# Modulation rows ahead of the input, values by pairs of token tiles, and input tiles read by grid rows

## The chip, the cores and the metric

The kernel runs on one core of one Trainium2 chip. Five engines work side by side, each through its own list of instructions in order: TensorE (PE; its weight loads are listed as PEld), VectorE (DVE), ScalarE (ACT), GpSimd (POOL) and SyncE (SP). Transfers are issued from SP's and ACT's lists and carried by 16 transfer engines. The metric is the time of one launch in microseconds.

## The reference, cut to what matters

The kernel does one step of a two-layer trunk: 512 latent tokens (a grid of 8 rows and 64 columns) and 128 context tokens, 1024 features. What the change touches is the start of layer 0: the modulation, the first norm and the projection to values.

```
def rmsnorm(x, g):
    y = x * lax.rsqrt(jnp.mean(x * x, axis=-1, keepdims=True) + EPS)
    return y * g

def adaln(cond, w, b):
    m = jax.nn.silu(cond) @ w + b
    return jnp.split(m[..., None, :], 6, axis=-1)

# layer 0: c for the latents, c_ctx for the context
sh, sc, ... = adaln(c, ada_w[0], ada_b[0])
h = rmsnorm(x, norm_mix_pre[0]) * (1.0 + sc) + sh
q, k, v = jnp.split(h @ na_w_qkv[0], 3, axis=-1)
```

Everything else (neighbourhood attention, the output projection, the FFN with its convolution, the second layer) is the same in both kernels.

## The kernel before, in words

The 640 tokens are five tiles of 128, x0 to x3 of latents and x4 of context. A latent tile holds 16 columns of the grid with all 8 rows, and a token's place in it is column times 8 plus row. `x_load` issues the load of a tile (512 KB, 128 partitions of 4 KB); `raw_ap` gives the source's counts and steps, from the outside in. `x_norm` squares the tile on ACT (with a sum), forms the reciprocal root on POOL in two small instructions and scales the tile on DVE. `x_turn` turns it on PE in eight transposes of 128x128 (`tr`), four to a PSUM bank; ACT copies the first bank to `xT` and DVE the second. `xT` has the features on the partitions in 8 chunks k, and 640 tokens along.

The modulation of the first norm (a scale and a shift of 1024 each) comes in four pieces i of two chunks k. `mod_load` loads a piece as four tiles `wf` of 512 KB; there are seven buffers `wf`, so the last tile of the third piece must wait until the second piece's first tile has been used, and the fourth piece for the rest. `mod_rows` multiplies (`row`), ACT copies the row (`rs`), and `mod_cols` turns it to columns on PE (`col`); three small instructions of DVE make the columns of scale and shift, `gcol` and `hcol`. Then for both k of the piece ACT writes scale times `xT` plus shift, rounded, to the high part `hT[0]`, DVE computes the same in full into `xT`, and DVE writes the difference to the low part `hT[1]`.

The values of the first four heads are `v_part(k, tiles)`: for a k and a tile three matmuls of 256 columns (high x high, high x low, low x high) into the tile's bank `vp`, for which `wv_load` loads half of the weights (512 KB, tile `wr`), ACT casts them (`wh`) and DVE subtracts (`wl`). Five `vp` banks of eight are held from the start.

PE's order is the order of the code, since `pe` ties each PE instruction to the one before it. The other engines' lists are set by a scheduler from the dependencies. In the kernel before SP issues x0, the constants (`const_loads`), x1 to x4, the first piece of modulation, the first value weights, pieces 2 and 3, the second value weights and piece 4. PE turns all five tiles, then does `row` and `col` of piece 1, `row` of piece 2, and then values, columns and rows in turn, until the weights of the queries and keys follow.

Of the kernel before, what the change touches and what calls it, by code (L numbers as in the profile page):

```python
# [104 lines left out]
def hybrid_step(ctx: ExitStack, tc: tile.TileContext, A, O):  # L105
# [13 lines left out]
    def turn(*a, **k):  # L119
        pe(nc.tensor.transpose(*a, **k))  # L120
# [4 lines left out]
    def f32(t):  # L125
        return t.bitcast(F32)
# [16 lines left out]
    cc = wp.tile([40, P], F32, tag="wr", name="cc")  # L143

    def const_loads():
        nc.sync.dma_start(cc[0:8, :], A["c"].rearrange("o (k p) -> (o k) p", p=P))
        nc.sync.dma_start(cc[8:16, :], A["c_ctx"].rearrange("(k p) -> k p", p=P))
        nc.sync.dma_start(cc[16:32, :], A["ada_b"][0, 0:2048].rearrange("(k p) -> k p", p=P))
        nc.sync.dma_start(cc[32:40, :], A["norm_mix_pre"][0].rearrange("(k p) -> k p", p=P))
        nc.sync.dma_start(ident, A["k_ident"])  # L150

    mhalf = cst.tile([P, 1], F32, name="mhalf")
    nc.gpsimd.memset(mhalf, -0.5)
    scolp = cst.tile([P, 2 * KC + 30], F32, name="scolp")
# [351 lines left out]
    with ExitStack() as s:  # L506
        sp = s.enter_context(pool("st"))
        xts = []

        def x_load(t):  # L510
            xt = sp.tile([P, D], F32, name=f"x0_{t}")
            if t < 4:
                nc.sync.dma_start(xt, raw_ap(A["x_sample"], 16 * t * D, [[D, 16], [GW * D, 8], [1, D]]))
            else:
                nc.sync.dma_start(xt, x_in(t))
            xts.append(xt)

        x_load(0)
        const_loads()
# [12 lines left out]
        gcol = sp.tile([P, KC, 2], F32, name="gcol")  # L532
        hcol = sp.tile([P, KC, 2], F32, name="hcol")

        def x_norm(t):
            xt = xts[t]
            ss = sm.tile([P, 1], F32, name="ss")
            junk = sp.tile([P, D], BF16, tag="junk", name="junk0")
            nc.scalar.activation(junk, xt, AF.Square, accum_out=ss)
            r = rstd_of(ss, D)  # L540
            nc.vector.tensor_scalar(xt, xt, r, None, op0=ALU.mult)

        def x_turn(t):
            for q in range(2):
                tr = bk.get("tr")
                tv = tr.rearrange("p (a b) -> p a b", a=4)
                for j in range(4):
                    turn(tv[:, j, :], xts[t][:, (4 * q + j) * P : (4 * q + j + 1) * P], ident)
                dst = xT[:, 4 * q : 4 * q + 4, t * P : t * P + P]
                if q:  # L550
                    nc.vector.tensor_copy(dst, tv)
                else:
                    nc.scalar.copy(dst, tv)
                bk.put(tr)

        def mod_load(i):
            out = {}
            for n in range(2):
                for h in range(2):
                    out[n, h] = sp.tile([P, 4, 256], F32, tag="wf", name="wf", bufs=7)  # L560
                    nc.sync.dma_start(out[n, h], rows(A["ada_w"][0], 4 * h, 4, D - D * n + 256 * i, 256))
            return out

        def mod_rows(i, ws):


            row = bk.get("row")
            for (n, h), w in ws.items():
                for j in range(4):
                    k = 4 * h + j  # L570
                    mm(row[32 * j : 32 * j + 32, 256 * n : 256 * n + 256], scolp[:, 2 * k : 2 * k + 32],
                       w[:, j, :], start=h == 0, stop=h == 1)
            rs = sp.tile([P, 512], F32, tag="rs", name="rs")
            nc.scalar.copy(rs, row)
            bk.put(row)
            return rs

        def mod_cols(i, rs):

            col = bk.get("col")  # L580
            for n in range(4):
                mm(col[:, 2 * n : 2 * n + 2], rs[:, n * P : n * P + P], sel, start=True, stop=True)
            cv = col[:, 0:8].rearrange("p (a b) -> p a b", b=2)
            ks = slice(2 * i, 2 * i + 2)

            def bc(c0):
# [3 lines left out]
            nc.vector.tensor_mul(gcol[:, ks, :], gcol[:, ks, :], bc(16))  # L590
            nc.vector.tensor_add(hcol[:, ks, :], cv[:, 2:4, :], bc(0))
            bk.put(col)
            for k in (2 * i, 2 * i + 1):
                for q, cs in ((0, slice(0, NS)), (1, slice(NS, T))):
                    g1, h1 = gcol[:, k, q : q + 1], hcol[:, k, q : q + 1]
                    i0 = nc.scalar.activation(hT[0][:, k, cs], xT[:, k, cs], AF.Identity, bias=h1, scale=g1)
                    nc.vector.tensor_scalar(xT[:, k, cs], xT[:, k, cs], g1, h1, op0=ALU.mult, op1=ALU.add)
                i1 = nc.vector.tensor_sub(hT[1][:, k, 0:T], xT[:, k, :], f32(hT[0][:, k, 0:T]))
            normed[:] = i0, i1

        vts_of[0] = na_v_tile()
        loads, wv = {}, {}

        def wv_load(i):
            wv[i] = wsplit(rows(wqkv, 4 * i, 4, 2048, 256), 4, 256)

        def x_in_norm(ts):
            for t in ts:
                if t:
                    x_load(t)  # L610
                x_norm(t)

        x_in_norm(range(NT))
        loads[0] = mod_load(0)
        wv_load(0)
        loads[1] = mod_load(1)
        loads[2] = mod_load(2)
        wv_load(1)
        loads[3] = mod_load(3)
        na_v_cache(vts_of[0], 0)  # L620
        vb = [bk.get("vp") for _ in range(NT)]

        def v_part(k, cs):
            for c in cs:
                wh, wl = wv[k // 4]
# [12 lines left out]
        rs = mod_rows(2, loads[2])  # L638
        v_part(2, range(3))
        mod_cols(2, rs)  # L640
        v_part(2, range(3, NT))
        v_part(3, range(NT))
        rs = mod_rows(3, loads[3])
        v_part(4, range(3))
        mod_cols(3, rs)
        v_part(4, range(3, NT))
        v_part(5, range(NT))
# [1314 lines left out]
```

## Time and profile before

| | |
|---|---|
| median of 3 runs | 1548.12 us (1547.24 to 1548.54) |
| span of the profiled execution | 1546.0 us |
| median less span | 2.1 us |
| PE busy | 1512.8 us, 98% |
| DVE, ACT, POOL busy | 66%, 55%, 45% |
| moved by the transfer engines | 243.99 MB, mean 158 GB/s |

The page gives no time of its own for the profiled execution beside its span from the first to the last instruction; what lies around the span is the 2.1 us to the median of the runs. Times in the profile are counted in us from the span's start. In a row of the timeline stand start, length, engine, line, operation, what is written and read, how many instructions were merged (x), and in brackets how long the engine had been idle and who ended that. L117 and L120 are the helpers through which all matmuls and transposes go, so the tile's name tells what is done. In a group of instructions the busy time and the mean of one in ns stand behind the bar. "Under 512 B" in a row on packets counts packets of that size or smaller steps up to the next limit; loads of 4 KB rows have one packet for each row.

### The profile page before, as it was taken

Reading aid. Unit: us, or ns where it says so; the run is one execution under the profiler, and the core shown is the slowest. Engines: PE = TensorE matmul, PEld = TensorE weight load, DVE = VectorE, ACT = ScalarE, POOL = GpSimd, SP = SyncE. Lnnn points to the kernel's source line nnn. Section 1 sums busy time; section 2 is a strip of 40 time slices with the busy share of each in tenths; the row PEclk is TensorE's granted clock in tenths of the full one; section 3 lists DMA queues with packets and bytes.
Section 4 is the critical chain, followed back from the end, with each engine's and each line's share of the span. In section 5 each row is a group of like instructions: output and inputs, shape, how many; then the busy total and the mean of one; then the engine's idle time right before and its main releaser. Section 6 shows DMA issues by size and latency. Waiting matters only on the chain.

```text
span 1546.0 us, 26097 instructions
## 1 busy us (share of the span) xinstructions
PE 1512.8 (98%) x9709; PEld 1344.4 (87%) x9709; DVE 1024.1 (66%) x1648; ACT 854.2 (55%) x1624; POOL 701.8 (45%) x606
## 2 busy tenths in 40 slices
PE   6999999999999999999999999999999999999998
PEld 5988998888999999978887878878899999988886
DVE  4553453659877666756757877773988887786554
ACT  5665564646655555654544447763666655554443
POOL 1554463432355455525444464532235666542433
PEclk9999999999999999999999999999999999999999
DMA  9745454253565665388574421015433334447664
GB/s 318 210 122 159 122 132 116 64 190 124 183 224 177 221 190 162 114 277 272 178 234 155 129 69 42 2 40 190 153 114 115 119 111 156 132 164 252 226 221 131
DMA packets 196666, 243.99 MB, mean 158 GB/s; under 512 B 11484, under 2 KB 153020, under 8 KB 196540
## 3 DMA queue, kind: packets, MB, share of 16 engines
q1 hardware_dynamic: 186704, 235.74, 47.7%
q10 hardware_dynamic: 9836, 6.59, 2.5%
q8 instruction: 76, 1.25, 0.3%
q14 instruction: 50, 0.41, 0.1%
HBM read 214.38 MB, written 26.34 MB: 156 GB/s over the span
## 4 chain that ended last, share of the span: by engine, by line
PE 66%; DVE 5%; ACT 2%; issue 2%; POOL 1%; DMA 1%; POOLq 0%; DVEq 0%; ACTq 0%
PE acc L117 19%; PE ux L117 18%; PE uz L117 8%; PE gp L117 5%; PE uy L117 4%; PE po L117 3%; PE y L117 3%; PE s L117 2%; PE tp L120 2%; PE ada L117 1%; DMA wr<-in_ffn_w_up 1%; DVE t L1281 1%; ACT gp L1692 1%; PE tr L120 0%; DVE xo L400 0%
## 5 line engine op out<-in xcount | busy, mean ns | idle before, releaser
L180 POOL TENSOR_TENSOR wl<-wr,wh 128x1024 fp32r<-128x1024 f32 x70 | 173.3, 2480 | 238.5 <-ACT wh L178 223.5
L1204 POOL TENSOR_TENSOR wl<-wr,wh 128x1024 fp32r<-128x1024 f32 x76 | 183.5, 2435 | 46.9 <-ACT wh L1203 43.3
L117 PE MATMUL ux<-B,wh 128*128 128x322 f32 x832 | 200.1, 311 | 0.9 <-ACT u L1258 0.9
L1281 DVE SCALAR_TENSOR_TENSOR t<-C,cw,t 128x644 f32<-128x644 f32 x176 | 156.3, 888 | 51.3 <-ACT t L1279 50.7
L117 PE MATMUL acc<-wh,alo 128*128 128x512 f32 x440 | 172.3, 392 | 0.3 <-DVE alo L1173 0.3
L178 ACT CAST wh<-wr 128x1024 fp32r<-128x1024 f32 x140 | 145.6, 1048 | 48.5 <-DMA wr<-in_ffn_w_down 37.4
L117 PE MATMUL acc<-wh,ahi 128*128 128x512 f32 x440 | 171.9, 391 | 0.0
L117 PE MATMUL acc<-wl,ahi 128*128 128x512 f32 x440 | 171.8, 391 | 0.0
L117 PE MATMUL uz<-B,wh 128*128 128x322 f32 x640 | 156.2, 312 | 0.9 <-ACT v L1258 0.9
L117 PEld LDWEIGHTS ux<-B,wh 128*128 128x128 f32 x832 | 143.6, 189 | 3.4 <-issue 1.2
L1173 DVE TENSOR_TENSOR alo<-ain,ahi 128x384 fp32r<-128x384 f32 (+1 forms) x88 | 84.0, 973 | 84.9 <-ACT ahi L1171 84.0
L117 PE MATMUL ux<-B,wl 128*128 128x322 f32 x416 | 129.5, 311 | 2.7 <-DVE wl L1204 2.7
L117 PE MATMUL qk<-hT,wh 128*128 128x384 f32 (+1 forms) x512 | 122.4, 315 | 0.0
L117 PEld LDWEIGHTS uz<-B,wh 128*128 128x128 f32 x640 | 110.9, 189 | 4.3 <-ACT v L1258 1.5
L1204 POOL TENSOR_TENSOR vl<-wr,vh 128x1024 fp32r<-128x1024 f32 x38 | 96.3, 2535 | 24.6 <-ACT vh L1203 24.3
L1203 ACT CAST wh<-wr 128x1024 fp32r<-128x1024 f32 x84 | 84.8, 1049 | 40.8 <-DVE wr L1227 40.5
L1279 ACT ACTIVATE t<-C,cw 128x644 f32<-128x644 f32 x88 | 78.6, 893 | 47.8 <-DVE C L1309 40.3
L180 DVE TENSOR_TENSOR wl<-wr,wh 128x1024 fp32r<-128x1024 f32 x70 | 91.3, 1315 | 20.1 <-ACT wh L178 19.5
L117 PE MATMUL uz<-B,wl 128*128 128x322 f32 x320 | 99.6, 311 | 0.3 <-POOL wl L1204 0.3
L117 PEld LDWEIGHTS acc<-wh,alo 128*128 128x128 f32 x440 | 82.5, 188 | 18.8 <-DVE alo L1173 1.1
L117 PEld LDWEIGHTS acc<-wl,ahi 128*128 128x128 f32 x440 | 82.6, 188 | 17.9
L117 PEld LDWEIGHTS acc<-wh,ahi 128*128 128x128 f32 x440 | 82.6, 188 | 17.8
(259 smaller groups left out, 3857.7 us busy)
## 6 DMA issues: line engine op xcount, KB each, us to landing
wr<-in_ffn_w_up SPq DMA_DIRECT2D x88, 512.0 KB
wr<-in_ffn_w_down SPq DMA_DIRECT2D x88, 512.0 KB
wr<-in_ada_w SPq DMA_DIRECT2D x72, 512.0 KB
act<-act SPq DMA_DIRECT2D x44, 321.0 KB
wr<-in_na_w_qkv SPq DMA_DIRECT2D x24, 512.0 KB
mod<-modrow SPq DMA_DIRECT2D x20, 512.0 KB
ain<-act SPq DMA_DIRECT2D x44, 192.0 KB
wf<-in_ada_w SPq DMA_DIRECT2D x16, 512.0 KB
```

What stands on the lines that cost most here:

```text
L117: pe(nc.tensor.matmul(*a, **k))
L120: pe(nc.tensor.transpose(*a, **k))
L178: i = nc.scalar.copy(hi, raw)
L180: j = (low or nc.vector).tensor_sub(lo, raw, f32(hi))
L1173: pin(nc.vector.tensor_sub(lo[:, 0 : c1 - c0], ain[:, 0 : c1 - c0], f32(hi[:, 0 : c1 - c0])))
L1203: nc.scalar.copy(hl[0], src)
L1204: low.tensor_sub(hl[1], src, f32(hl[0]))
L1279: nc.scalar.activation(t, taps(0), AF.Identity, bias=cw[:, 3, n : n + 1], scale=cw[:, 1, n : n + 1])
L1281: nc.vector.scalar_tensor_tensor(t, taps(d), cw[:, w, n : n + 1], t, op0=ALU.mult, op1=ALU.add)
L1692: nc.scalar.activation(self.pt[i].rearrange("p (a b) -> p a b", a=2), sv, AF.Exp, bias=nm, scale=-1.0, accum_out=su)
```

## The change

Three things are changed.

- The loads of the constants move from SP's to ACT's list, to its very start. SP begins with the first piece of modulation, then x0, x1, the first value weights, x2, x3, x4; the rest follows as it was. `row` and `col` of piece 1 stand ahead of the first turn.
- A latent tile is read by grid rows: 8 rows of the grid outside, 16 columns inside, so 64 KB lie together in the source, and a token's place in the loaded tile is row times 16 plus column. The turn writes its columns with a step of 8 to bring the former order back.
- `mod_cols` ends with `gcol` and `hcol`; what follows is `mod_apply(i, parts)`, which can be done for a range of tokens. For piece 1 it is done for tiles 0 and 1, 2 and 3, and 4, and the value matmuls of k = 0 and 1 follow by these groups. Pieces 2 to 4 are applied whole. A `vp` bank is taken when its tile's first value matmul is due.

On PE the list begins with one product for the constants and the five tiles' turns; then come the first two `row`:

```order
L120 MATMUL ct<-ident,cc 128x40
L120 MATMUL tr<-ident,x_0_134 128x128 x8
...
L120 MATMUL tr<-ident,x_4_193 128x128 x8
L117 MATMUL row<-wf,scolp 32x256 x16
L117 MATMUL col<-sel,rs 128x2 x4
L117 MATMUL row<-wf,scolp 32x256 x16
L117 MATMUL vp<-wh,hT_122 128x256
```

The same place in the changed kernel:

```order
L120 MATMUL ct<-ident,cc 128x40
L117 MATMUL row<-wf,scolp 32x256 x16
L117 MATMUL col<-sel,rs 128x2 x4
L120 MATMUL tr<-ident,x_0_161 128x8x16 x8
L120 MATMUL tr<-ident,x_1_171 128x8x16 x8
L120 MATMUL tr<-ident,x_2_187 128x8x16 x8
L117 MATMUL vp<-wh,hT_127 128x256
...
L120 MATMUL tr<-ident,x_3_197 128x8x16 x8
L120 MATMUL tr<-ident,x_4_207 128x128 x8
L117 MATMUL vp<-wh,hT_127 128x256
...
L117 MATMUL row<-wf,scolp 32x256 x16
L117 MATMUL col<-sel,rs 128x2 x4
L117 MATMUL row<-wf,scolp 32x256 x16
```

The first `row` and `col` moved ahead of the turns. Twelve value matmuls (tiles 0 and 1) stand between turn 2 and turn 3, and eighteen (tiles 2, 3 and 4) between turn 4 and the second `row`. Behind that `row` come its `col` and the third `row` with no value matmul between them.

ACT's list in the changed kernel, from the first copied row on; `junk,ss` is the square of a tile, `xT` the copy of half a turned tile, `wh` the cast of the value weights:

```order
L574 COPY rs<-row 128x512
L538 ACTIVATE junk_164,ss<-x_0_161 128x1024
L538 ACTIVATE junk_174,ss<-x_1_171 128x1024
L553 COPY xT<-tr 128x4x128
L179 CAST wh<-wr 128x1024
L553 COPY xT<-tr 128x4x128
L538 ACTIVATE junk_190,ss<-x_2_187 128x1024
L602 ACTIVATE hT_127<-xT,hcol,gcol 128x256 x2
L538 ACTIVATE junk_200,ss<-x_3_197 128x1024
L553 COPY xT<-tr 128x4x128
L538 ACTIVATE junk_210,ss<-x_4_207 128x1024
L553 COPY xT<-tr 128x4x128
```

In the kernel before, the squares of x0 to x2 stood one behind the other, and the cast behind all five turns and the first copied row. Now the square of x2 stands behind the copies of turns 0 and 1 and the cast.

DVE's list in the changed kernel, behind the scaling of x3 and x4: the copies of turns 3 and 4, and between and behind them what `mod_apply` does for tiles 2, 3 and 4:

```order
L551 COPY xT<-tr 128x4x128
L603 TENSOR_SCALAR xT<-xT,gcol,hcol 128x256
L551 COPY xT<-tr 128x4x128
L604 TENSOR_TENSOR hT_128<-xT,hT_127 128x256
L603 TENSOR_SCALAR xT<-xT,gcol,hcol 128x256
L603 TENSOR_SCALAR xT<-xT,gcol,hcol 128x128
L604 TENSOR_TENSOR hT_128<-xT,hT_127 128x256
L604 TENSOR_TENSOR hT_128<-xT,hT_127 128x128
L603 TENSOR_SCALAR xT<-xT,gcol,hcol 128x128
L604 TENSOR_TENSOR hT_128<-xT,hT_127 128x128
```

In the kernel before, this work was four pieces and two of 640 columns, in whole rows behind `gcol`, which came after all turns. Seven of these pieces now follow the copy of turn 4.

The diff, cut to its core:

```
     def const_loads():
-        nc.sync.dma_start(cc[0:8, :], A["c"].rearrange("o (k p) -> (o k) p", p=P))
...
-        nc.sync.dma_start(ident, A["k_ident"])
-
+        nc.scalar.dma_start(cc[0:8, :], A["c"].rearrange("o (k p) -> (o k) p", p=P))
...
+        nc.scalar.dma_start(ident, A["k_ident"])
+
+    const_loads()
...
             if t < 4:
-                nc.sync.dma_start(xt, raw_ap(A["x_sample"], 16 * t * D, [[D, 16], [GW * D, 8], [1, D]]))
+                nc.sync.dma_start(xt, raw_ap(A["x_sample"], 16 * t * D, [[GW * D, 8], [D, 16], [1, D]]))
...
                 for j in range(4):
-                    turn(tv[:, j, :], xts[t][:, (4 * q + j) * P : (4 * q + j + 1) * P], ident)
+                    out = tv[:, j, :].rearrange("p (c r) -> p r c", r=8) if t < 4 else tv[:, j, :]
+                    turn(out, xts[t][:, (4 * q + j) * P : (4 * q + j + 1) * P], ident)
...
             bk.put(col)
+
+        def mod_apply(i, *parts):
+
             for k in (2 * i, 2 * i + 1):
-                for q, cs in ((0, slice(0, NS)), (1, slice(NS, T))):
-                    g1, h1 = gcol[:, k, q : q + 1], hcol[:, k, q : q + 1]
-                    i0 = nc.scalar.activation(hT[0][:, k, cs], xT[:, k, cs], AF.Identity, bias=h1, scale=g1)
-                    nc.vector.tensor_scalar(xT[:, k, cs], xT[:, k, cs], g1, h1, op0=ALU.mult, op1=ALU.add)
-                i1 = nc.vector.tensor_sub(hT[1][:, k, 0:T], xT[:, k, :], f32(hT[0][:, k, 0:T]))
+                for c0, c1 in parts:
+                    for q, cs in ((0, slice(c0, min(c1, NS))), (1, slice(max(c0, NS), c1))):
+                        if cs.start >= cs.stop:
+                            continue
...
+                    i1 = nc.vector.tensor_sub(hT[1][:, k, c0:c1], xT[:, k, c0:c1], f32(hT[0][:, k, c0:c1]))
...
-        x_in_norm(range(NT))
         loads[0] = mod_load(0)
+        x_in_norm(range(2))
         wv_load(0)
+        x_in_norm(range(2, NT))
         loads[1] = mod_load(1)
...
-        for t in range(NT):
+        def v_pair(cs):
+            for k in range(2):
+                v_part(k, cs)
+
+        mod_cols(0, mod_rows(0, loads[0]))
+        for t in range(3):
             x_turn(t)
-        rs = mod_rows(0, loads[0])
-        mod_cols(0, rs)
+            if t == 1:
+                mod_apply(0, (0, 256))
+        v_pair((0, 1))
+        for t in range(3, NT):
+            x_turn(t)
+            mod_apply(0, (256, NS) if t < 4 else (NS, T))
+        v_pair((2, 3))
+        v_pair((4,))
+        whole = (0, T)
         rs = mod_rows(1, loads[1])
-        v_part(0, range(2))
         mod_cols(1, rs)
-        v_part(0, range(2, NT))
-        v_part(1, range(NT))
...
+        mod_apply(1, whole)
+        for i in (2, 3):
+            rs = mod_rows(i, loads[i])
+            v_part(2 * i - 2, range(3))
+            mod_cols(i, rs)
+            mod_apply(i, whole)
+            v_part(2 * i - 2, range(3, NT))
+            v_part(2 * i - 1, range(NT))
```

More of the change, by code (lines that the diff above doesn't have):

```diff
@@ L145, in const_loads @@
     def const_loads():
-        nc.sync.dma_start(cc[0:8, :], A["c"].rearrange("o (k p) -> (o k) p", p=P))
-        nc.sync.dma_start(cc[8:16, :], A["c_ctx"].rearrange("(k p) -> k p", p=P))
-        nc.sync.dma_start(cc[16:32, :], A["ada_b"][0, 0:2048].rearrange("(k p) -> k p", p=P))
-        nc.sync.dma_start(cc[32:40, :], A["norm_mix_pre"][0].rearrange("(k p) -> k p", p=P))
-        nc.sync.dma_start(ident, A["k_ident"])
+        nc.scalar.dma_start(cc[0:8, :], A["c"].rearrange("o (k p) -> (o k) p", p=P))
+        nc.scalar.dma_start(cc[8:16, :], A["c_ctx"].rearrange("(k p) -> k p", p=P))
+        nc.scalar.dma_start(cc[16:32, :], A["ada_b"][0, 0:2048].rearrange("(k p) -> k p", p=P))
+        nc.scalar.dma_start(cc[32:40, :], A["norm_mix_pre"][0].rearrange("(k p) -> k p", p=P))
+        nc.scalar.dma_start(ident, A["k_ident"])
+    const_loads()
     mhalf = cst.tile([P, 1], F32, name="mhalf")
@@ L516, in x_load @@
             xts.append(xt)
-        x_load(0)
-        const_loads()
         sel = sp.tile([P, 2], F32, name="sel")
@@ L592, in mod_cols @@
             bk.put(col)
+        def mod_apply(i, *parts):
             for k in (2 * i, 2 * i + 1):
-                for q, cs in ((0, slice(0, NS)), (1, slice(NS, T))):
-                    g1, h1 = gcol[:, k, q : q + 1], hcol[:, k, q : q + 1]
-                    i0 = nc.scalar.activation(hT[0][:, k, cs], xT[:, k, cs], AF.Identity, bias=h1, scale=g1)
-                    nc.vector.tensor_scalar(xT[:, k, cs], xT[:, k, cs], g1, h1, op0=ALU.mult, op1=ALU.add)
-                i1 = nc.vector.tensor_sub(hT[1][:, k, 0:T], xT[:, k, :], f32(hT[0][:, k, 0:T]))
+                for c0, c1 in parts:
+                    for q, cs in ((0, slice(c0, min(c1, NS))), (1, slice(max(c0, NS), c1))):
+                        if cs.start >= cs.stop:
+                            continue
+                        g1, h1 = gcol[:, k, q : q + 1], hcol[:, k, q : q + 1]
+                        i0 = nc.scalar.activation(hT[0][:, k, cs], xT[:, k, cs], AF.Identity, bias=h1, scale=g1)
+                        nc.vector.tensor_scalar(xT[:, k, cs], xT[:, k, cs], g1, h1, op0=ALU.mult, op1=ALU.add)
+                    i1 = nc.vector.tensor_sub(hT[1][:, k, c0:c1], xT[:, k, c0:c1], f32(hT[0][:, k, c0:c1]))
             normed[:] = i0, i1
@@ L608, in x_in_norm @@
             for t in ts:
-                if t:
-                    x_load(t)
+                x_load(t)
                 x_norm(t)
-        x_in_norm(range(NT))
         loads[0] = mod_load(0)
+        x_in_norm(range(2))
         wv_load(0)
+        x_in_norm(range(2, NT))
         loads[1] = mod_load(1)
@@ L620, in hybrid_step @@
         na_v_cache(vts_of[0], 0)
-        vb = [bk.get("vp") for _ in range(NT)]
+        vb = {}
         def v_part(k, cs):
             for c in cs:
+                if k == 0:
+                    vb[c] = bk.get("vp")
                 wh, wl = wv[k // 4]
@@ L627, in v_part @@
                        (wh[:, k % 4, :], wl[:, k % 4, :]), k == 0, k == KC - 1)
-        for t in range(NT):
-            x_turn(t)
-        rs = mod_rows(0, loads[0])
-        mod_cols(0, rs)
+        def v_pair(cs):
[3 more added lines that the diff above has]
+        for t in range(3):
+            x_turn(t)
+            if t == 1:
[7 more added lines that the diff above has]
+        whole = (0, T)
         rs = mod_rows(1, loads[1])
-        v_part(0, range(2))
         mod_cols(1, rs)
-        v_part(0, range(2, NT))
-        v_part(1, range(NT))
[L638 to L647, printed above, removed]
+        mod_apply(1, whole)
[6 more added lines that the diff above has]
+            v_part(2 * i - 1, range(NT))
         crs = []
```

## The prediction

> **What bounds the kernel now.** I read the page first, then the busy time by stretches of the start, then the timeline of the first 50 us, then the transfers there.
>
> ```profile
> span 1546.0 us, 26097 instructions
> PE 1512.8 (98%) x9709; PEld 1344.4 (87%) x9709; DVE 1024.1 (66%) x1648; ACT 854.2 (55%) x1624; POOL 701.8 (45%) x606
> ...
> 9.60:21.40 11.80, 9.64 (x44) 7.91 (x48) 5.58 (x8) 6.80 (x13) 3.46 (x9) 1.00 1.06 330
> 21.40:30.50 9.10, 7.12 (x87) 4.42 (x87) 5.28 (x11) 4.29 (x7) 0.00 (x0) 1.00 1.09 383
> 30.50:50.80 20.30, 20.30 (x204) 17.99 (x204) 13.95 (x32) 12.07 (x21) 1.87 (x4) 1.00 0.92 258
> 50.80:74.00 23.20, 23.20 (x159) 23.17 (x158) 11.30 (x32) 14.07 (x33) 16.78 (x15) 1.00 0.76 226
> ```
>
> PE is busy for 98% of the span. In a row of the stretches the first pair of numbers is the stretch and its length, then come PE, PEld, DVE, ACT and POOL, the granted clock, the share of the transfer engines and GB/s. PE has holes before 30.5 us and none from there to 74 us. So a shift of the first value stage is carried on by a full PE, one us for one us, and only the first 40 us need be worked out. The edge that I follow is the last modulation product (the fourth `row`, which starts at 40.02): behind it the order of PE is the same in both kernels.
>
> ```profile
> 6.33 1.06 ACT L539 ACTIVATE junk<-x 128x1024 bf16<-128x1024 f32 x1 [3.02 <-DMA x<-in_x_sample]
> 9.08 1.06 ACT L539 ACTIVATE junk<-x 128x1024 bf16<-128x1024 f32 x1 [0.51 <-DMA x<-in_x_sample]
> 9.65 1.97 PE L120 MATMUL tr<-ident,x 128*128 128x128 f32 x8 [1.30 <-DVE x L541]
> 11.19 0.75 DVE L541 TENSOR_SCALAR x<-x,rstd 128x1024 f32<-128x1024 f32 x1 [1.59 <-POOL rstd L206]
> 11.30 1.06 ACT L539 ACTIVATE junk<-x 128x1024 bf16<-128x1024 f32 x1 [1.06 <-DMA x<-in_x_sample]
> 17.77 3.64 PE L120 MATMUL tr<-ident,x 128*128 128x128 f32 x16 [1.54 <-DVE x L541]
> 18.89 0.59 ACT L553 COPY xT<-tr 128x512 f32<-128x512 f32 x1 [1.84 <-PE tr L120]
> 24.30 1.05 PE L117 MATMUL col<-sel,rs 128*128 128x2 f32 x8 [0.71 <-ACT rs L574]
> 25.28 2.28 PE L117 MATMUL row<-wf,scolp 128*32 128x256 f32 x32
> 30.87 0.16 DVE L590 TENSOR_TENSOR gcol<-gcol,colb 128x4 f32<-128x4 f32 x1
> 31.05 0.28 PE L117 MATMUL vp<-wl,hT 128*128 128x256 f32 x1
> 31.40 0.28 PE L117 MATMUL vp<-wl,hT 128*128 128x256 f32 x1
> 32.76 0.82 DVE L598 TENSOR_TENSOR hT<-xT,hT 128x640 fp32r<-128x640 f32 x1
> 33.52 1.93 PE L117 MATMUL row<-wf,scolp 128*32 128x256 f32 x32
> 35.57 0.59 ACT L574 COPY rs<-row 128x512 f32<-128x512 f32 x1 [2.21 <-PE row L117]
> 40.02 1.93 PE L117 MATMUL row<-wf,scolp 128*32 128x256 f32 x32
> ```
>
> From these: a tile's square on ACT starts at 9.08, its scaling on DVE at 11.19, that is 2.11 later; with 0.75 for the scaling PE can turn the tile 2.9 us after ACT took it up. A turn is 1.95 of PE; ACT copies its first half about 1.1 after it starts. Three value matmuls (one tile, one k) take 31.40 - 31.05 = 0.35.
>
> **The change, part by part.** The loads first. A tile of 512 KB of x was in use every 11.30 - 9.08 = 2.22 us. Three stretches of the transfers show why that is slow, and two show into how many shares a load is cut:
>
> ```profile
> DMA packets 319, 1.18 MB, mean 235 GB/s; under 512 B 32, under 2 KB 32, under 8 KB 319
> q1 hardware_dynamic: 319, 1.18, 103.5%
> ...
> DMA packets 110, 0.40 MB, mean 401 GB/s; under 512 B 12, under 2 KB 12, under 8 KB 110
> q1 hardware_dynamic: 110, 0.40, 99.6%
> ...
> 16.00:38.00 22.00, 18.49 (x182) 14.20 (x181) 12.05 (x28) 10.39 (x18) 1.24 (x3) 1.00 1.09 385
> ...
> DMA packets 295, 0.31 MB, mean 208 GB/s; under 512 B 72, under 2 KB 240, under 8 KB 295
> ...
> DMA packets 84, 0.08 MB, mean 56 GB/s; under 512 B 8, under 2 KB 84, under 8 KB 84
> ```
>
> The first pair is 6 to 11 us, loads of x: 287 packets of 4 KB fill 103.5% of 16 engines for 5 us, 288 ns each. The second is 106 to 107 us, where rows of 4 KB of `ada_w` arrive: 98 packets, 163 ns each. The rows of x that follow each other lie 256 KB apart in the kernel before, those of `ada_w` 24 KB. In the change 16 rows follow each other without a gap, so I take 163 ns, with 288 as the other bound. From 16 to 38 us the modulation and value weights come at 385 GB/s, 0.524/385 = 1.36 us for a load.
>
> Each load ends with small packets, its marks of completion: 32 for the two that end between 6 and 11 us. From 4 to 5.5 us there are 72, which is 16 for x, 16 for `ident`, 16 for the 16 rows of `ada_b` and 8 each for the three loads of 8 rows. The last row (45.6 to 46.95 us) holds the end of one bias load of 64 rows, whose source counts 8 outside and 8 inside: 8 marks. So a load is cut by the outer count of its source. In the kernel before that count is 16 for x, now it is 8: I take it that 8 engines carry 16 rows each, 16 x 0.163 = 2.6 us for a tile, not 16 engines with 8 rows (1.3). The gain of the shorter packet is spent on the halved engines. No load of 128 rows with an outer count of 8 stands in this trace, so 1.3 stays the lower bound and 16 x 0.288 = 4.6 the upper.
>
> The Trainium skill (DMA: Bandwidth & Descriptors, "Why a DMA increments its semaphore by 16 and not by 1") has a rule for it: the number of engines is the largest up to 16 that divides the outer counts of both sides. By it x runs on 8 engines and the sum is the one below; without it, it is that of the third case. The marks above agree. The same page ("Latency and other measured facts") lists row pitches: at 512 KiB it still measured 207 of 214 GB/s, by which the pitch of 256 KB would cost next to nothing. This trace has 235 against 401 GB/s, so the row decides.
>
> Then the order. Ahead of x0 now stand the four loads of the first modulation: x0 is in use at 6.33 + 4 x 1.36 + (2.6 - 2.22) = 12.2, x1 at 14.8, x2 at 18.8 (the value weights stand between), x3 at 21.4, x4 (16 engines) at 22.7. The constants move to ACT's queue and land while that modulation is on its way, and the first row and column products are done before x0: 2.2 + 1.0 of PE that leave the path. Durations for what follows:
>
> ```profile
> L180 DVE TENSOR_TENSOR wl<-wr,wh 128x1024 fp32r<-128x1024 f32 x4 | 4.8, 1219 | 0.0
> L178 ACT CAST wh<-wr 128x1024 fp32r<-128x1024 f32 x4 | 4.1, 1042 | 0.0
> L120 PE MATMUL tr<-ident,x 128*128 128x128 f32 x40 | 9.6, 426 | 3.4 <-DVE x L541 3.4
> L551 DVE COPY xT<-tr 128x512 f32<-128x512 f32 x5 | 3.5, 690 | 3.1 <-PE tr L120 3.1
> L553 ACT COPY xT<-tr 128x512 f32<-128x512 f32 x5 | 2.9, 582 | 3.6 <-PE tr L120 3.6
> ```
>
> x0 is turned from 15.1 (9.65 before) to 17.05; x1, squared at 14.8, from 17.7 to 19.65. On ACT the square of x2 now stands behind the cast of the value weights and the copy of turn 1: 18.7 + 0.6 = 19.3, though x2 is there at 18.8; so turn 2 is 22.2 to 24.15. PE does the pair 0, 1 (12 matmuls, 1.4) to 25.6. DVE scales x3 only behind the copy of turn 2 (24.2 + 0.7), so turn 3 starts at 25.7 and turn 4 ends at 29.6. Behind turn 4 DVE has its copy (to 30.35) and seven pieces of 256 or 128 columns. With 0.82 for 640 columns and 1.22 for 1024 a column costs 1.04 ns, so 0.42 and 0.29 to 0.32 each, 2.5 together: 32.85. The last value products of the first two k wait for them; the second `row` starts at 33.0 (25.28 before).
>
> From there to the fourth `row`: product 1.9, copy 0.1 + 0.6, column 1.05, columns of gain 0.4, so 4.1; the low part of hT for the next k follows 2.55 later (from 30.87 + 0.16 to 32.76 + 0.82), at 6.6. In the kernel before, 0.35 x 10 = 3.5 us of value products stood here and filled this wait; they have been used up, and only the third `row` is left (1.93). Then nine matmuls less what ran already (0.85), column 0.95, 21 matmuls 2.5: 10.9. The fourth `row` starts at 33.0 + 10.9 = 43.9.
>
> A check by sums: PE work from the first turn to that edge is 9.6 + 2 x 1.93 + 2 x 0.95 less overlap 0.1 + 60 x 0.117 = 22.3; 15.1 + 22.3 = 37.4, and the walk has 0.65 + 2.55 + 0.1 + 1.3 + 0.85 + 0.95 = 6.4 of idle PE.
>
> The buffers. SP waits in order:
>
> ```profile
> 15.01 11.33 SPq L561 DMA_DIRECT2D wf<-in_ada_w  x8
> 26.40 0.73 SPq L174 DMA_DIRECT2D wr<-in_na_w_qkv  x1
> 27.22 7.37 SPq L561 DMA_DIRECT2D wf<-in_ada_w  x4
> ```
>
> Seven buffers hold eight loads, so the last load of the third modulation waits for the second `row`: it ended at 26.34, 1.06 behind the start of that product. In the change it goes out at 34.1, with the second value weights, the fourth modulation and the q/k weights behind it on SP. Six loads of 1.36 and 1.2 to start make 33.0 + 1.06 + 1.2 + 8.2 = 43.4: half a us before PE wants them. It costs nothing as long as PE's own walk is that long, and is what is late next.
>
> Costed at nothing: the moved constants (ACT issues five loads, 0.3 each, with 6 us of cover before its first result is wanted; without cover 1.5); the turns' outputs with a step of 8 (245 ns for 128 columns, against 117 for 256 in a value product, so a slot has four times the room; if they took double, 4 x 1.95 more).
>
> **Sum.** 43.9 - 40.0 = +3.9. The profiled span of 1546.0 becomes 1549.9; the median of the timed runs, 1548.12, lies 2.1 over that span, so 1552.0.
>
> **Rivals.** *The rows of x stay slow* at 288 ns on 8 engines, since their eight streams still lie 256 KB apart: x0 at 14.2, x3 at 29.4, turn 4 ends at 36.2, the second `row` at 39.6: +10.5, 1558.6. For it: the same bytes are asked for in the same 512 KB. Against: each stream is now contiguous.
>
> *16 engines, 163 ns*: x0 at 10.9, x2's square still behind turn 1, at 17.4, the second `row` at 31.1: +2.0, 1550.1, which a measurement would call no change (0.2% is 3.1 us).
>
> *Faster*: 16 engines and a PE that doesn't idle. The place is PE's wait ahead of turn 2 and of the second `row`: the point that decides is a second `row` before 29.1. Without any idle PE the edge is 13.8 + 22.3 = 36.1, -3.9, 1544.2. With 8 engines it can't come: x4 at 22.7 and thirteen loads of 1.36 put the fourth modulation at 40.4. Against it stand ACT's and DVE's orders above.
>
> **How the numbers follow.** Forecast 0.56 (its own range 1549.5 to 1555.5), slow rows 0.17, 16 engines 0.17, faster 0.10. Range 1547.5 to 1559.0: it takes in the first three cases. Faster by over 0.2%: 0.07 (most of the last case); within: 0.36 (the third case, a third of the forecast, the rest of the last); slower: 0.57.
>
> **What would show it.** In the changed profile: 8 small packets for each of x0 to x3; squares at 12.2, 14.8, 19.3; first turn at 15.1; second `row` at 33.0 and fourth at 43.9; PE full behind it. It is wrong if x tiles come every 1.3 or 4.6 us, if the second `row` starts before 29, or if PE has idle time behind 50 us that takes the shift back.

## The result, and the profile after

The median went from 1548.12 us (5 runs, 1547.24 to 1548.68) to 1557.79 us (5 runs, 1556.32 to 1559.94): slower by a ratio of 1.0066, interval 1.0054 to 1.0079. By the medians that is +9.7 us. The forecast was +3.9; +9.7 lies in the range on record but outside the forecast's own (1549.5 to 1555.5), and next to the rival whose rows of x stay slow (+10.5).

The page of the changed kernel, to be set beside the two lines shown of before:

```profile
span 1556.7 us, 26108 instructions
PE 1513.8 (97%) x9709; PEld 1345.4 (86%) x9709; DVE 1025.9 (66%) x1654; ACT 853.8 (55%) x1626; POOL 699.8 (45%) x606
```

PE does the same 9709 instructions in a busy time 1.0 us longer, while the span is 10.7 us longer: nearly all of the loss is PE waiting. Where it waits, the stretches tell (columns as in the prediction: stretch, PE, PEld, DVE, ACT, POOL, granted clock, share of the transfer engines, GB/s):

```profile
16.00:24.00 8.00, 2.78 (x12) 2.38 (x13) 2.37 (x4) 2.56 (x4) 1.44 (x4) 0.50 0.86 196
24.00:32.00 8.00, 4.89 (x24) 4.49 (x23) 5.06 (x9) 5.39 (x10) 1.55 (x5) 0.50 0.82 250
38.36:49.45 11.09, 9.69 (x111) 7.41 (x111) 5.89 (x16) 6.38 (x11) 0.00 (x0) 1.00 0.89 295
49.45:61.64 12.19, 11.02 (x110) 9.59 (x109) 8.08 (x17) 6.17 (x12) 1.89 (x5) 1.00 0.91 200
61.64:90.00 28.36, 28.14 (x196) 27.86 (x195) 14.64 (x41) 17.17 (x40) 22.01 (x22) 1.00 0.69 197
```

From 16 to 32 us PE works 7.7 of 16 us, and its row gives a granted clock of 0.50. The transfer engines are marked as busy 82 to 86% of it and yet move only 196 to 250 GB/s. From 61.64 on PE is full again. The squares on ACT show what PE is waiting for:

```profile
14.70 1.06 ACT L538 ACTIVATE junk<-x 128x1024 bf16<-128x1024 f32 x1 [1.41 <-DMA x<-in_x_sample]
20.28 1.06 ACT L538 ACTIVATE junk<-x 128x1024 bf16<-128x1024 f32 x1 [4.43 <-DMA x<-in_x_sample]
25.37 1.06 ACT L538 ACTIVATE junk<-x 128x1024 bf16<-128x1024 f32 x1 [0.44 <-DMA x<-in_x_sample]
29.17 1.06 ACT L538 ACTIVATE junk<-x 128x1024 bf16<-128x1024 f32 x1 [1.67 <-DMA x<-in_x_sample]
```

Each of the four latent tiles is awaited from its load, and they come 5.6, 5.1 and 3.8 us apart. In the kernel before the first three came 2.75 and 2.22 us apart; the forecast had 2.6, with the value weights once between. PE's own timeline carries this to the edge that the prediction followed:

```profile
9.04 3.60 PE L117 MATMUL row<-wf,scolp 128*32 128x256 f32 x32 [0.69 <-DMA wf<-in_ada_w]
...
17.62 1.97 PE L120 MATMUL tr<-ident,x 128*128 128x128 f32 x8 [3.22 <-DVE x L540]
23.19 1.97 PE L120 MATMUL tr<-ident,x 128*128 128x128 f32 x8 [3.60 <-DVE x L540]
28.27 1.97 PE L120 MATMUL tr<-ident,x 128*128 128x128 f32 x8 [3.11 <-DVE x L540]
...
32.60 2.15 PE L120 MATMUL tr<-ident,x 128*128 128x128 f32 x16
...
38.36 1.93 PE L117 MATMUL row<-wf,scolp 128*32 128x256 f32 x32
...
49.45 1.50 PE L117 MATMUL row<-wf,scolp 128*32 128x256 f32 x24
52.12 0.64 PE L117 MATMUL row<-wf,scolp 128*32 128x256 f32 x8 [1.17 <-DMA wf<-in_ada_w]
...
61.64 0.28 PE L117 MATMUL qk<-hT,wh 128*128 128x256 f32 x1
```

The first product of the queries and keys, in the kernel before:

```profile
50.81 0.28 PE L117 MATMUL qk<-hT,wh 128*128 128x256 f32 x1
```

So the fourth `row` starts at 49.45 in place of 40.02 (+9.4); its last quarter waits 1.17 more for its weights; the queries and keys start 10.8 later, and the span is 10.7 longer. What is lost by 62 us stays lost.

The transfers while x comes (10 to 13 and 22 to 26 us), and at 38 to 40 us, with SP's issue of the third piece's loads behind them:

```profile
DMA packets 301, 0.52 MB, mean 172 GB/s; under 512 B 9, under 2 KB 230, under 8 KB 301
q1 hardware_dynamic: 301, 0.52, 102.0%
...
DMA packets 165, 0.64 MB, mean 161 GB/s; under 512 B 8, under 2 KB 8, under 8 KB 165
q1 hardware_dynamic: 165, 0.64, 50.7%
...
DMA packets 108, 0.10 MB, mean 52 GB/s; under 512 B 7, under 2 KB 108, under 8 KB 108
...
13.35 26.07 SPq L561 DMA_DIRECT2D wf<-in_ada_w  x8
```

From 22 to 26 us x is alone. It fills half of the 16 engines (50.7%), and its load ends with 8 marks: it does run on 8 engines. 157 packets of 4 KB in 0.507 x 64 = 32.4 engine-us are 207 ns each. From 10 to 13 us other packets (1 KB, rows of weights) run beside it. All 16 engines are full, and together they move 172 GB/s, where the kernel before moved 235 with its column reading and 385 with weights alone. From 38 to 40 us nearly nothing is moved: the last load of the third piece waits on SP for the second `row`, as the prediction said.

### The profile page after: what moved, and what is told of

Its sections match the earlier page's. It is cut to its first block, busy times and chain, and to the rows that moved or that the text cites. A ratio compares the mean times of both kernels' runs of the same rounds, so it can differ in the third digit from the quotient of the medians.

```text
span 1556.7 us, 26108 instructions
## 1 busy us (share of the span) xinstructions
PE 1513.8 (97%) x9709; PEld 1345.4 (86%) x9709; DVE 1025.9 (66%) x1654; ACT 853.8 (55%) x1626; POOL 699.8 (45%) x606
## 4 chain that ended last, share of the span: by engine, by line
PE 66%; DVE 5%; ACT 2%; issue 2%; POOL 1%; DMA 1%; POOLq 0%; DVEq 0%; ACTq 0%
PE acc L117 19%; PE ux L117 18%; PE uz L117 8%; PE gp L117 5%; PE uy L117 4%; PE po L117 2%; PE y L117 2%; PE s L117 2%; PE tp L120 2%; PE ada L117 1%; DMA wr<-in_ffn_w_up 1%; DVE t L1296 1%; ACT gp L1707 1%; PE tr L120 0%; DVE xo L401 0%
## 5 line engine op out<-in xcount | busy, mean ns | idle before, releaser
L1296 DVE SCALAR_TENSOR_TENSOR t<-C,cw,t 128x644 f32<-128x644 f32 x176 | 156.4, 889 | 51.3 <-ACT t L1294 50.7
L117 PEld LDWEIGHTS acc<-wh,alo 128*128 128x128 f32 x440 | 82.6, 188 | 18.8 <-DVE alo L1188 1.1
```

The source lines that it names most:

```text
L117: pe(nc.tensor.matmul(*a, **k))
L1296: nc.vector.scalar_tensor_tensor(t, taps(d), cw[:, w, n : n + 1], t, op0=ALU.mult, op1=ALU.add)
```

## The experiments

**The two halves apart.** The first run is the changed kernel with x read by columns again, so that the new order stands alone:

```
-  ... raw_ap(A["x_sample"], 16 * t * D, [[GW * D, 8], [D, 16], [1, D]])
+  ... raw_ap(A["x_sample"], 16 * t * D, [[D, 16], [GW * D, 8], [1, D]])
-  out = tv[:, j, :].rearrange("p (c r) -> p r c", r=8) if t < 4 else tv[:, j, :]
-  turn(out, ...)
+  turn(tv[:, j, :], ...)
```

> The changed kernel with one part undone: the latent tiles are read by columns again (16 outside, 8 rows inside), and the turn writes in plain order. In the changed kernel the five tiles were in use at 14.7, 20.3, 25.4, 29.2 and 30.7 us and the second row product started at 38.4. Theory A, the reading order costs most of it: tiles every 2.2 us again, in use at about 11.8, 14.0, 17.6, 19.8 and 21.6, second row product at 32 to 33, +3 to +5 us against the kernel before. Theory B, the order of the work costs it all, whatever the loads do: +8 to +10. Theory C, the order costs nothing: within 1 us of the kernel before.

The second is the kernel before with this edit the other way round, so that the new reading stands alone.

> The kernel before with the reading by grid rows alone (load and turn), the order of the work as it was. Theory A: 4 KB packets of about 350 ns on 8 engines, 5 us for a latent tile in place of 2.2, so x4 and all loads behind it come some 11 us later: +9 to +12 us. Theory B: under +4, since the loads are not what the time went to.

PE's timeline of the first, then of the second:

```profile
31.99 1.93 PE L117 MATMUL row<-wf,scolp 128*32 128x256 f32 x32
...
43.09 1.93 PE L117 MATMUL row<-wf,scolp 128*32 128x256 f32 x32
53.90 0.28 PE L117 MATMUL qk<-hT,wh 128*128 128x256 f32 x1
```

```profile
46.01 1.93 PE L117 MATMUL row<-wf,scolp 128*32 128x256 f32 x32
56.80 0.28 PE L117 MATMUL qk<-hT,wh 128*128 128x256 f32 x1
```

The order alone: 1552.75 against 1548.87, ratio 1.0030 (1.0019 to 1.0042), +3.9, as its theory A had it. The reading alone: 1554.72, ratio 1.0042 (1.0029 to 1.0054), +5.9. Their sum, +9.7, is that of the whole change. Both parts cost, the reading more. The second run came out between its two expectations (+9 to +12, or under +4): its tiles of x were squared 4.0, 4.8 and 4.3 us apart, but there the modulation's loads queue behind x, and the values still fill PE while pieces 2 to 4 arrive. That is the likely reason why its fourth `row` was 6.0 late and not 9; it was not tested alone.

**The forecast's own conditions.** Two runs take x in rows that lie next to each other, which makes other tokens of each tile and leaves the work as it is: one as 128 rows, so that 16 engines carry a tile; one with an outer count of 8, whose streams are 16 rows, 64 KB, apart.

```
-  ... raw_ap(A["x_sample"], 16 * t * D, [[GW * D, 8], [D, 16], [1, D]])
+  ... x_in(t)
```

```
+  ... raw_ap(A["x_sample"], 128 * t * D, [[16 * D, 8], [D, 16], [1, D]])
```

> The changed kernel with each latent tile loaded as 128 neighbouring rows (outer count 128), so the tiles hold other tokens than they should. Theory A: packets of 160 ns on 16 engines, 1.3 to 1.5 us for a tile, in use at about 10.9, 12.3, 15.0, 16.4 and 17.8; the second row product at about 31, because the work on ACT, DVE and PE and no load sets it: +2 to +3 us. Theory B: +8 or more. Theory C: faster than the kernel before by 1 us or more.

> As the run with 128 neighbouring rows, but the source counted as 8 outside and 16 inside, without a gap: 8 streams that start 64 KB apart in place of 256 KB. The tokens are others than they should be. If the halved number of engines is what slows the packets: 300 ns or more for 4 KB and a time like the changed kernel's, +8 to +10. If it is the distance of 256 KB between the eight streams: 160 ns, 2.6 us for a tile on 8 engines, tiles in use at 12.2, 14.8, 18.8, 21.4 and 22.7 and +3.9 us, which are the conditions that the forecast had assumed.

The run on 8 engines: PE's timeline, and its transfers from 10 to 12 us, with those of the changed kernel at the same time behind them.

```profile
16.64 3.67 PE L120 MATMUL tr<-ident,x 128*128 128x128 f32 x16 [1.19 <-DVE x L540]
22.89 1.97 PE L120 MATMUL tr<-ident,x 128*128 128x128 f32 x8 [2.57 <-DVE x L540]
...
27.21 2.26 PE L120 MATMUL tr<-ident,x 128*128 128x128 f32 x16
...
33.16 1.93 PE L117 MATMUL row<-wf,scolp 128*32 128x256 f32 x32
...
44.26 1.50 PE L117 MATMUL row<-wf,scolp 128*32 128x256 f32 x24
46.22 0.64 PE L117 MATMUL row<-wf,scolp 128*32 128x256 f32 x8 [0.46 <-DMA wf<-in_ada_w]
...
55.73 0.28 PE L117 MATMUL qk<-hT,wh 128*128 128x256 f32 x1
```

```profile
DMA packets 347, 0.79 MB, mean 397 GB/s; under 512 B 24, under 2 KB 196, under 8 KB 347
q1 hardware_dynamic: 347, 0.79, 102.0%
...
DMA packets 231, 0.38 MB, mean 191 GB/s; under 512 B 1, under 2 KB 183, under 8 KB 231
q1 hardware_dynamic: 231, 0.38, 109.2%
```

Both have 4-KB rows of x beside 1-KB rows of weights on full engines; here they move 397 GB/s, in the changed kernel 191. The second `row` starts at 33.16 and the fourth at 44.26, where the forecast had 33.0 and 43.9; the time is 1552.15, ratio 1.0028 (1.0017 to 1.0039), where it had 1552.0 (+3.3 over its own runs of the kernel before, for a forecast of +3.9; the trace is of an execution of 1553.86). So 8 engines are not what makes the tiles late. That the second `row` comes within 0.2 of the forecast is in part luck, since errors of both signs lie between: the first turn is 1.5 late (16.64 against 15.1) and so is turn 3 (27.21 against 25.7); the twelve value products ahead of turn 3 take 2.70 (24.51 to 27.21) where the forecast had 1.4; and then turns 3 and 4 take 2.26 together where it had 3.9. With 16 engines the second `row` starts at 32.44 and the time is 1551.83 (1.0029, 1.0018 to 1.0041): no measurable gain over 8. In both runs no square waits for a load, and ACT holds x0: its square (13.43 and 13.76) stands behind the copy of the first row (12.95 and 13.28). The late constants and the slow first product, 3.64 and 3.58 in place of the 1.93 of later ones, show only when x is early.

**How far apart the streams may lie.** Three runs change only the distance of the eight streams; from 64 rows (256 KB) to 63 (252 KB, the diff), to 32 (128 KB) and to 50 (200 KB); the tokens are others again.

```
-  ... raw_ap(A["x_sample"], 16 * t * D, [[GW * D, 8], [D, 16], [1, D]])
+  ... raw_ap(A["x_sample"], 16 * t * D, [[63 * D, 8], [D, 16], [1, D]])
```

> The changed kernel with the eight rows of a latent tile 252 KB apart in place of 256 KB (tokens others than they should be). If the power of two between the eight streams slows them: 160 ns for a packet of 4 KB, tiles in use at 13, 15, 19, 22 and 24, and a time like that of the eight neighbouring streams (+3 to +5 us). If it is the distance as such, pages far apart: 350 ns, tiles in use as in the changed kernel and +8 to +10.

> The changed kernel with the eight streams of an x tile 128 KB apart (32 rows) in place of 256 KB; the tokens are others, the work is the same. Theory A (what slows a tile is the distance of its eight streams, and 64 KB was fast, 252 and 256 KB slow): at 128 KB the 4-KB packets take something between 159 and 350 ns; if the distance works by degrees, about 250 ns, with squares of x every 3.5 us and the second row at about 35.5. Theory B (only streams that span most of the 2 MB of x are slow): 159 ns as with neighbouring rows, second row at 33 to 33.5. Theory C (every distance of 128 KB or more is slow once other packets run beside): 300 ns and more while rows of the weights arrive, 160 to 200 alone, second row at 37 to 38.5.

> The changed kernel with the eight streams 200 KB apart (50 rows); the tokens are others. Theory C (any large distance is slow beside other packets): second row at 37 to 38.5 as with 252 KB. Theory A (by degrees): between the runs with 128 and with 252 KB. If 128 KB is slow and 200 KB fast, it is the power of two after all, with 252 KB too near to one.

The second `row` started at 37.65 with 252 KB, at 37.24 with 200 KB and at 37.06 with 128 KB (64 KB: 33.16; 256 KB: 38.36). The times: 1559.18 for 252 KB (ratio 1.0071, 1.0054 to 1.0088); 1556.9 in the one run each of the other two, beside 1548.14. The transfers of the 128-KB run, first beside the weights (10 to 12 us), then with x alone (23 to 25 us):

```profile
DMA packets 233, 0.39 MB, mean 197 GB/s; under 512 B 7, under 2 KB 180, under 8 KB 233
q1 hardware_dynamic: 233, 0.39, 111.0%
...
DMA packets 107, 0.42 MB, mean 211 GB/s; under 512 B 4, under 2 KB 4, under 8 KB 107
q1 hardware_dynamic: 107, 0.42, 51.8%
```

Alone, the 103 packets of 4 KB take 0.518 x 32 / 103 = 161 ns each, the 163 of `ada_w` in the prediction. Beside the weights all 16 engines are full and the sum is no larger: 197 GB/s. So beside the weights it is neither the power of two (252 and 200 KB are slow too) nor a packet that is slower in itself: from 10 to 12 us both together move 191 (256 KB), 210 (252 KB), 216 (200 KB) and 197 GB/s (128 KB) on full engines. The theory that matched is the third, "beside other packets". With x alone it differs: at 256 KB a packet takes 207 ns, at 252 KB 161 (99 packets, 23 to 25 us):

```profile
DMA packets 105, 0.41 MB, mean 203 GB/s; under 512 B 6, under 2 KB 6, under 8 KB 105
q1 hardware_dynamic: 105, 0.41, 49.8%
```

The 252-KB run thus met neither expectation whole: its packets alone are as fast as the first had it, its tiles and its time (+10.8) as late as the second, or a little later.

The Trainium skill (DMA: Bandwidth & Descriptors, "Latency and other measured facts") finds a loss only at large powers of two, and a few KB of padding as the cure. With x alone the runs agree: 207 ns a packet at 256 KB, 161 at 252. Beside the weights they don't: 4 KB less brought 191 only to 210 GB/s, far from the 397 at 64 KB, and there the measurement decides. At 64 KB a tile is also one block of 512 KB without gaps, so the runs don't part the distance from the gaps, and they don't tell why 64 KB is fast and 128 KB is not.

**Row first.** With columns read, the second `row` is put ahead of the values of tiles 2 to 4, so that these fill its copy's wait again:

```
-  v_pair((2, 3))
-  v_pair((4,))
   rs = mod_rows(1, loads[1])
+  v_pair((2, 3))
   mod_cols(1, rs)
   mod_apply(1, whole)
+  v_pair((4,))
```

> The changed kernel read by columns, and the second row product stands ahead of the values of tiles 2, 3 and 4, its columns between those of tiles 2, 3 and of tile 4. If the order costs because the value products are used up before the second row product and leave its copy, columns and modulation uncovered: the second row product at about 28.5, the fourth at 40 to 41, that is 2 to 3 us better than with columns alone (43.1) and within 1.5 us of the kernel before. If the cost is the late and staggered norm of the tiles: no better than with columns alone, +3 to +5 us.

```profile
30.14 1.93 PE L117 MATMUL row<-wf,scolp 128*32 128x256 f32 x32
...
35.22 1.93 PE L117 MATMUL row<-wf,scolp 128*32 128x256 f32 x32
...
41.88 1.93 PE L117 MATMUL row<-wf,scolp 128*32 128x256 f32 x32
```

1550.43, ratio 1.0012 (1.0004 to 1.0021): the fourth `row` 1.2 earlier than in the first run, and 1.9 behind the kernel before. That is better than columns alone and still less than expected: the second `row` was to start at 28.5 and the fourth at 40 to 41, and the time was to lie within 1.5 us of the kernel before, where it is 2.1 us above it. The fillers used up too early were a real part of the cost of the order; the rest was not taken apart.

**The constants.** Again with columns read, the five loads go back to SP, ahead of the first piece of modulation:

```
-  nc.scalar.dma_start(cc[0:8, :], ...)
+  nc.sync.dma_start(cc[0:8, :], ...)
...
-  nc.scalar.dma_start(ident, A["k_ident"])
+  nc.sync.dma_start(ident, A["k_ident"])
```

> The changed kernel with x read by columns and a plain turn, as in the first experiment, and the five loads of constants back on SP's list, ahead of the first load of the modulation. In the first experiment ident landed at 7.97 behind the modulation's packets, the first row took 3.64 from 8.99, and the square of x0 stood behind its copy at 13.17. Theory A (the late constants hold the start): ct at about 5, the first row follows its weights and is copied at about 11, the square of x0 when it lands at about 12; turn 4 one to one and a half us earlier, second row at 30.5 to 31, fourth at 41.5 to 42, against 31.99 and 43.09. Theory B (the loads set the start; five issues of 0.3 to 0.5 on SP put the modulation back by 1.9): ct early, but squares 0.5 to 1.5 later than the first experiment's where ACT waits for a load, second row at 32.5 to 33.5. Prediction of the first experiment's size, 1552 to 1553.5, is B's; 1551 to 1551.5 is A's.

```profile
6.48 1.08 PE L117 MATMUL row<-wf,scolp 128*32 128x256 f32 x8 [1.97 <-DMA wf<-in_ada_w]
...
12.29 1.08 PE L117 MATMUL row<-wf,scolp 128*32 128x256 f32 x8 [1.11 <-DMA wf<-in_ada_w]
...
34.49 1.93 PE L117 MATMUL row<-wf,scolp 128*32 128x256 f32 x32
```

The constants come early, and now the first product waits for its weights instead, to 13.4. The square of x0 moves from 13.17 to 14.50 and the second `row` from 31.99 to 34.49; the time is 1554.36, ratio 1.0039 (1.0024 to 1.0053). So with the constants early the loads set the start; the second `row` came 1 us later than even that theory had said, and the time 0.9 us above its range. Of these two places for the constants ACT's list is the better one.

**A busy start.** The run with 16 engines for x gets 36 products of zeros on PE ahead of the constants' turn.

```
+  fill = bk.get("fill")
+  for _ in range(36):
+      mm(fill[:, 0:256], fz[:, 0:P], fz, start=True, stop=True)
+  bk.put(fill)
   ct = bk.get("ct")
```

> The run with 128 neighbouring rows on 16 engines (tokens others than they should be), with 36 products of a zero tile on PE ahead of the constants' turn, from about 1 us on. If the first row product took 3.6 us there because PE had stood idle: 1.9 us now, the square of x0 at about 12 in place of 13.8, the second row product at 30 to 31 in place of 32.4, and 1 to 2 us less than that run. If it took 3.6 us because its weights arrived one by one: no change.

```profile
1.18 17.62 PE L117 MATMUL fill<-fz 128*128 128x256 f32 x72 [1.18 <-POOL fz L522]
...
19.84 1.94 PE L117 MATMUL row<-wf,scolp 128*32 128x256 f32 x32 [0.85 <-DVE scolp L535]
```

The 36 products are 72 in the trace and held PE for 17.6 us, to 18.8, far longer than meant, and the kernel was slower for it (1554.99, ratio 1.0043, 1.0030 to 1.0055). One thing can be read all the same: behind a busy PE the first `row` takes 1.94, against 3.58 in the same kernel without the zeros. By then the weights had long landed, so the run alone doesn't part the busy PE from weights in place. Two rows shown above do: a quarter of a `row` (x8) that starts when its weights land took 1.08 at 12.29 in the run with the constants on SP, and 0.64 at 52.12 in the changed kernel. So the first product is slow because PE works at about half rate there, not because its weights come one by one.

**Fast reading in the old order.** The kernel before takes x as 128 neighbouring rows and puts the tokens in order in the copies out of PSUM:

```
-  ... raw_ap(A["x_sample"], 16 * t * D, [[D, 16], [GW * D, 8], [1, D]])
+  ... x_in(t)
+  if t < 4:
+      dst = xT[:, 4 * q : 4 * q + 4, 0:NS].rearrange("p k (c r) -> p k r c", r=8)[:, :, 2 * t : 2 * t + 2, :]
+      tv = tv.rearrange("p a (r c) -> p a r c", r=2)
```

> The kernel before, in its own order of work, but each latent tile is loaded as 128 neighbouring tokens (two whole grid rows, outer count 128), and the copies from PSUM into xT put every token at column times 8 plus row. If the reading alone is worth something: packets of 160 ns, tiles in use every 1.4 us, at about 5.5, 6.9, 8.2, 9.6 and 11, the first row product at 18 to 19 in place of 21.3, the fourth at 36 to 38 in place of 40.0: -2 to -4 us against the kernel before. If PE's own work from the first turn on sets the edge, or the copies with a step of 8 cost as much as the loads save: within 1 us.

Its groups of copies (before: 690 and 582 ns):

```profile
L554 DVE COPY xT<-tr 128x512 f32<-128x512 f32 x5 | 5.1, 1013 | 2.0 <-PE tr L120 2.0
L556 ACT COPY xT<-tr 128x512 f32<-128x512 f32 x5 | 4.8, 997 | 2.1 <-PE tr L120 2.1
```

1548.45 against 1548.38, ratio 1.0002 (0.9993 to 1.0011): no change. The tiles didn't come every 1.4 us: x0 and x1 were squared earlier (5.35 and 7.43, against 6.33 and 9.08), but x2 waited for its load to 11.33 (11.30 before), and x3 and x4 were squared at 14.18 and 16.36 (13.86 and 15.90 before). The copies with steps took about 1.0 each, PE waited for them, and the second `row` started at 25.86, against 25.28 before. So the run doesn't show what the fast reading would be worth without those copies. No kernel tried here beats the kernel before.

## Why the prediction was right or wrong

**Right: the sign, the place and the path.** The loss has arisen by the end of the fourth `row`, and behind 61.64 PE is full and gives nothing back. The size was missed by 5.8 us; the range holds the result only because it was drawn to take in the rival with slow rows. From the second to the fourth `row` the forecast had 10.9; it took 11.09. The loads are cut into 8 shares.

**Wrong: the price of a tile.** The step that failed is "in the change 16 rows follow each other without a gap, so I take 163 ns", 2.6 us a tile. The pair of rows that it rested on (288 ns for x, 163 for `ada_w`) differed in the distance of rows within an engine's share and in the distance of what the engines read at the same time; I credited all to the former. The runs show that the latter counts: eight streams 64 KB apart run at 397 GB/s with weights beside them, eight streams 256 KB apart at 191 at the same time. This made the second `row` 5.4 late against the forecast (38.36 against 33.0), and 5.2 against the run with 64 KB (33.16). x3 itself was in use 7.8 late (29.17 against 21.4); the walk had 1.4 of slack ahead of turn 3, and from turn 3 to the second `row` it took 5.8 (38.36 - 32.60) where the forecast had 7.3. The rival with slow rows named this cause, with 0.17 where it should have had more: its ground ("their eight streams still lie 256 KB apart") was in the working. Its x0 at 14.2 and x3 at 29.4 stand against 14.70 and 29.17, its second `row` at 39.6 against 38.36; even so its 288 ns on 8 engines was not the measure, but the rate of all engines together.

**Wrong: the spare half microsecond.** The forecast let the fourth modulation land 0.5 ahead of need and called it "what is late next". PE waited 1.17 for its last quarter in the change, and 0.46 in the run that met the forecast's conditions. The chain was right (the buffers, SP's wait, the idle transfers), but its sum of loads was too short: the last quarter was there 13.8 (52.12 - 38.36) and 13.1 (46.22 - 33.16) behind the second `row`, where the forecast had 10.4. That the last quarter is wanted only 1.5 behind the start of the product took up part of it.

**Costed at nothing.** The turns' outputs with a step of 8: right. Eight took 1.97 at 17.62 as they did at 9.65 in the kernel before, and the last two turns 2.15 together, as against 2.18 with plain outputs in the run with the row first. The constants: right for this kernel, since x0 (14.70) is later than the copy of the first row (12.71), but not for the reason given. They landed at 8, behind the weights, not under cover; in the runs with 16 engines for x and with streams 64 KB apart they and the slow first product held the square of x0 to 13.76 and 13.43. The forecast had that product at 2.2 and early.

**Not foreseen: the clock.** "A turn is 1.95 of PE" holds only at half rate. Turns 0 to 2 took 1.97 each with 0.50 in their rows, turns 3 and 4 took 2.15 together (32.60), 1.8 less than the forecast's 3.9. The turns of the kernel before, from which the 1.95 was read, took as long as those at 0.50, although their rows say 1.00. Against that stand the twelve value products of tiles 0 and 1, which took 32.60 - 29.89 = 2.7 us at 0.50, against 1.4. Since x3, taken up at 29.17, could be turned from 32.07 at the earliest by the prediction's 2.9, the path lost only 0.5 by them. In the run with streams 64 KB apart the two errors nearly cancel (2.70 for 1.4, 2.26 for 3.9).

Together: 3.9 (forecast) + 5.4 (second `row`) + 0.2 (to the fourth) + 1.2 (its last quarter) = 10.7, the difference of the spans.

One of the prediction's sums is off: its chances for "within" and "slower" (0.36 and 0.57) don't follow from the parts named, which give 0.17 + 0.56/3 + 0.03 = 0.39 and leave 0.54.

## What to carry to other kernels

Before a load is reshaped, write down for each engine which addresses it reads and how far these lie from what the others read at the same moment; a contiguous stream for each engine says nothing about their sum, and the price must be measured with the traffic that will run beside it. Moving work ahead of its input also uses it up as filler: look at which wait it covered before. When two rows of a profile differ in two ways, neither difference may be priced from them alone. And a duration holds only for the rate at which the engine worked there: compare equal instructions along the trace before one of them becomes a price.

## What the runs showed of the hardware that was not expected

- Eight streams of contiguous 4-KB rows: 64 KB apart, 397 GB/s beside weights; 128 KB apart, 161 ns a packet alone (211 GB/s on half the engines) but only 197 GB/s in all on full engines beside weights; 252 KB apart, 161 ns alone and 210 GB/s beside weights; 256 KB apart, 207 ns alone and 191 GB/s beside weights (172 from 10 to 13 us).
- Granted clock 0.50 from 16 to 32 us, with PE idle 3.22, 3.60 and 3.11 us ahead of three turns. The Trainium skill (TensorE: Matmul & The Clock Gate, Part 1) gives half rate after an idle window of about 3.4 us, counted from a point that the kernel does not set; the trace is near that. The row of the clock and the rate don't always agree at the start of a trace: with streams 64 KB apart the rows say 1.00 from 24 to 26 us, and yet the twelve value products took 2.70 us there, as at 0.50 in the changed kernel (2.7). That trace holds no record of the clock ahead of 27.93 us, so its 1.00 before that says nothing of the rate.
- A turn of eight fp32 transposes took 1.97 at half rate, and 1.07 to 1.10 at full rate (32.60, 2.15 for two, in the changed kernel; 22.67, 1.10 for one, with the order alone). The first `row` of the new order took 3.58 to 3.77 in the eight traces where it ran in one piece behind an idle PE, and 1.94 behind the zeros.
